# The queries' length as a scale of the scores: forget-bias and latent heads of a three-block transformer

## The chip, the cores and the metric

The kernel runs on one core of a Trainium2 chip. The metric is the device time of one launch in microseconds (us), as the median of several runs. A core has a matrix engine (TensorE, PE), a vector engine (VectorE, DVE), a scalar engine (ScalarE, ACT), a general engine (GpSimd, POOL) and a queue engine that issues the DMAs here (SyncE, SP). The engines run side by side and wait for one another through semaphores.

## The reference

Three blocks work on 512 tokens of width 1024 in fp32. The first is an even mixer (eight forget-bias heads and eight chunked heads with a relative bias) with an MLP, the second an odd mixer (eight stick-breaking heads and eight latent heads) with an MLP, the third a hybrid mixer with a gated MLP. The change touches the forget-bias heads of the first block and the latent heads of the second. Both work on inputs that an RMS norm has scaled token by token:

```python
def rmsnorm(x, g):
    y = x * rsqrt(mean(x * x, axis=-1) + EPS)     # one factor per token
    return y * g

# forget-bias heads: h = rmsnorm(x, norm_mix), q = h @ Wq, k = h @ Wk
s = q @ k.T * HEAD_DIM ** -0.5
s = s + cum_q[:, None] - cum_k[None, :]           # cum: running sum of log forget gates
p = softmax(where(k_pos <= q_pos, s, -inf))
o = p @ v

# latent heads: q_full = rmsnorm(c_q, q_norm) @ w_uq, kv = rmsnorm(c_kv, kv_norm) @ w_ukv
s = (q_nope @ k_nope.T + rope(q_rope) @ rope(k_rope).T) * (NOPE_DIM + ROPE_DIM) ** -0.5
p = softmax(where(k_chunk <= q_chunk, s, -inf))   # chunks of 64 tokens
o = p @ v
```

The factor of the norm is one number for each token. In the scores it is one number for each row (the query's token) and one for each column (the key's token).

## The kernel before, in words

Activations lie feature-major, as tiles of 128 features by 512 tokens. Every fp32 operand of a matrix product is kept as a high and a low part (`wh`, `wl` of a weight, an `AB` pair of an activation), and a product is three passes: high by high, high by low, low by high. `split` (L574) makes such a pair: ACT copies the high part, and DVE subtracts it from the source to get the low part.

The norm's factor is not applied to the input of a projection but to its result. `rows` (L670) turns a column of factors, one per token, into a 128x512 tile that holds the factors along the tokens (`rbc`, and `rbcq` with the scores' scale in it): PE transposes the broadcast column, four times for 512 tokens, and ACT copies the result from PSUM. `scaled_pair` (L708) multiplies a projection's result in PSUM by that row on DVE, into a tile `G`, and splits `G` into a pair `AB`. There are two buffers `AB` and three `G`. SP then moves the pair by DMA to where the scores want it: `to_stack` (into `QS`), `to_dup` (into `KK`), and for the latent heads `mla_operands` (L1003, into tiles `h`, with the roped part `X` and the key's `krp` beside it).

`softmax` (L745) handles 128 queries at a time against 128, 256, 384 or 512 keys. PE makes the scores in PSUM (`pss`). One DVE instruction, the bias-and-maximum, adds the bias or mask (`strip`) to the scores and takes the extremum of each row (the scores are negated here, so it is a minimum); it shows in the trace as a custom instruction with a read of its accumulator behind it. ACT takes the exponential and its sum, DVE the reciprocal, and POOL multiplies by it (`x<-x,sm`). Then PE transposes the probabilities (`psp`), they are split (`pt`) and multiplied by the values (`pso`).

A forget-bias head makes its own bias (`fox_bias`, L890): PE transposes the running sums, ACT copies them, and for each block of queries POOL adds the query's sum, a per-partition pointer, and fills what lies above the diagonal (`affine_select`). A latent head has one mask for all (`chm`, L1043). `latent_rows` (L982) makes the rows of the latent keys and queries, lets POOL multiply the rope's cosine and sine tiles by the queries' row, and runs the rope's projection.

The order of the instructions is not the program's. Every operation is recorded, and a list scheduler (`schedule`, L391) places them by assumed costs (`cost`, L322) and latencies, with priority by place in the program; `later` and `fill` push pieces of other work (the latent inputs, half of an output projection) between the heads. A tile gets a buffer in the order in which the operations are placed (`BUFS`, L544; PSUM `PBUFS`, L546). All recorded operations are issued from one line, so the trace shows L372 for each of them, and groups are told apart by their tiles: `psg` is a projection's result, `wr` a weight as loaded, `sm` a small column of factors, sums or maxima, `L` and `o` the latent inputs of queries and keys.

Of the kernel before, what the change touches and what calls it, by code (L numbers as in the profile page):

```python
# [15 lines left out]
ALU = mybir.AluOpType  # L16
# [4 lines left out]
NT = 4  # L21
KD = 8
BIG = 1e30
# [479 lines left out]
class Net:  # L503
# [204 lines left out]
    def scaled_pair(self, ps, rbc):  # L708
        t = self.tl("G", [128, 512])
        self.nc.vector.tensor_tensor(t, ps, rbc, ALU.mult)  # L710
        ab = self.pair("AB")
        self.split(ab, t)
        return ab
# [31 lines left out]
    def softmax(self, i, passes, bias, gate=None):  # L745

        nc = self.nc
        n = 128 * (i + 1)
        s = self.scores(i, passes)
        p = self.tl("x", [128, 512])  # L750
        m = self.small(4)
        nc.vector.tensor_tensor_reduce(p[:, :n], s[:, :n], bias(i), scale=1.0, scalar=3e38,
                                       op0=ALU.add, op1=ALU.min, accum_out=m[:, 0:1])
        nc.scalar.activation(p[:, :n], p[:, :n], AF.Exp, scale=-1.0, bias=m[:, 0:1], accum_out=m[:, 1:2])
        nc.vector.reciprocal(m[:, 2:3], m[:, 1:2])
        if gate == "raw":
            return p, m[:, 2:3]
        nc.gpsimd.tensor_scalar(p[:, :n], p[:, :n], m[:, 2:3], 1.0 if gate is None else gate(i), ALU.mult, ALU.mult)
        return p
# [60 lines left out]
    def soft_head(self, passes, bias, v, dst, u, gate=None):  # L820
        ps_list = [self.softmax(i, passes, bias, gate) for i in range(NT)]
        pt = self.turn(ps_list)
        o = self.psum("o")
        self.av(o, pt, v)
        self.fold(o, dst, u)
# [36 lines left out]
    def even_mixer(self):  # L862
        nc = self.nc
        rbc, rbcq = self.finish_norm([("rbc", 1.0), ("rbcq", -0.125)])
# [19 lines left out]
        for a in range(NT):  # L884
            nc.tensor.matmul(ps[:, 8 * a:32], allones if a else tri, lf[:, 0:32 - 8 * a], start=(a == 0), stop=(a == NT - 1))
        cum, ncum = self.small(32), self.small(32)
# [3 lines left out]
        def fox_bias(hd):  # L890
# [7 lines left out]
            def bias(i):  # L898
                n = 128 * (i + 1)
                b = self.tl("strip", [128, 512])  # L900
                nc.gpsimd.tensor_scalar(b[:, :n], ck[:, :n], ncum[:, 8 * i + hd:8 * i + hd + 1], 1.0, ALU.add, ALU.mult)
                nc.gpsimd.affine_select(b[:, n - 128:n], b[:, n - 128:n], pattern=[[-1, 128]], compare_op=ALU.is_ge,
                                        fill=BIG, base=0, channel_multiplier=1)
                return b[:, :n]
# [11 lines left out]
        for kind, mk in (("fox", fox_bias), ("chk", chk_bias)):  # L916
            for t in range(4):
                if not (kind == "fox" and t == 0) and t % 2 == 0:
                    vt = self.v_tiles(f"{kind}_v{t // 2}", h, self.rcol)
                q, k = self.qk(f"{kind}_qk{t}", h, rbcq, rbc, "op" if kind == "fox" and t == 0 else "gg")  # L920
# [7 lines left out]
                for u in range(2):  # L928
                    passes = [(qs[:, u], kk[u][:, 0]), (qs[:, u], kk[u][:, 1])]
                    self.soft_head(passes, mk(2 * t + u), self.vhead(vt, 2 * (t % 2) + u), ob, u)  # L930
# [5 lines left out]
    def odd_mixer(self):  # L936
# [45 lines left out]
        def latent_rows():  # L982

            rkb, = self.rows(lat["rkv"], [("rbc", 1.0)])
            rqb, = self.rows(lat["rq"], [("rbcq", -(96.0 ** -0.5))])
            nc.gpsimd.tensor_tensor(C, C, rqb, ALU.mult)
            nc.gpsimd.tensor_tensor(S, S, rqb, ALU.mult)
# [8 lines left out]
            return rkb, rqb, hold["r"]  # L996
# [6 lines left out]
        def mla_operands(t):  # L1003
            q = qkd(f"uq_nope{t}", lat["cq"], rqb)
# [16 lines left out]
        for t in range(4):  # L1021
# [8 lines left out]
            if t == 3:  # L1030
                with self.rec.later(LATER):
                    vm = self.v_tiles("ukv_v0", lat["ckv"], lat["rkv"])
                    rkb, rqb, (r1, r2) = latent_rows()
# [11 lines left out]
        nc.gpsimd.memset(chm[0:64, 448:512], BIG)  # L1045
        for t in range(4):
# [4 lines left out]
            for u in range(2):  # L1051
                Q, K = pair[u]
                passes = [(Q[0:96, 0], K[0:96, 0]), (Q[0:96, 0], K[0:96, 1]), (Q[0:96, 1], K[0:96, 0])]
                self.soft_head(passes, lambda i: chm[:, 384 - 128 * i:512], self.vhead(vt, 2 * (t % 2) + u), ob, u)
# [736 lines left out]
```

## Time and profile before

| | |
|---|---|
| runs | 2073.0, 2075.69, 2075.41 us; median 2075.41 |
| profiled execution | 2075.91 us, of which the span from first to last instruction 2074.2 us |
| mean granted TensorE clock | 0.991 |
| TensorE matmuls | 2016.1 us, 97% of the span |
| TensorE weight loads | 1684.7 us, 81%, beside the matmuls |
| VectorE | 1134.4 us, 55% |
| ScalarE | 895.1 us, 43% |
| GpSimd | 394.3 us, 19% |

Busy time is a mean over the whole span. What matters for a change is the stretch in which it lies, and there which engine waits for which. In the rows below, a bracket at the end of a row gives how long the engine had been idle and what released it.

### The profile page before, as it was taken

The numbers are of one execution on the slowest core, as the hardware profiler recorded it, in microseconds if no ns is written. First come the engines' busy times: TensorE is split into PE (matmuls) and PEld (weight loads), VectorE is DVE, ScalarE is ACT, GpSimd is POOL, SyncE is SP. The second block draws the span as 40 slices with busy tenths as digits, with TensorE's granted clock in tenths as the row PEclk, the third lists the DMA queues.
The fourth block names the chain that finished last, engine by engine and source line by source line (L and its number), as shares of the span: only waits on it lengthen the run. The fifth ranks groups of instructions, "written<-read, shape, count | busy, mean of one in ns | idle before, by whom it ended". The sixth has DMA issues, their size and how long they took to land. (4 is left out here: it accounts for less than half of the span.)

```text
span 2074.2 us, 27227 instructions
## 1 busy us (share of the span) xinstructions
PE 2016.1 (97%) x9958; PEld 1684.7 (81%) x9958; DVE 1134.4 (55%) x2033; ACT 895.1 (43%) x1621; POOL 394.3 (19%) x524
## 2 busy tenths in 40 slices
PE   8999999999999998999999999989999999999998
PEld 7887778888888887878888888867788888888887
DVE  6657763434444677874434354766786644333334
ACT  5556542323344565652323253534685543222224
POOL 2343210000022453220000014212240221011013
PEclk9999999999999999999999999999999999999999
DMA  6545623233344325633333334464113222323232
GB/s 199 135 128 152 195 83 102 92 102 92 101 134 132 102 62 130 194 101 96 97 100 94 102 120 141 119 174 126 60 42 112 92 101 92 102 92 102 91 102 82
DMA packets 80677, 231.98 MB, mean 112 GB/s; under 512 B 11552, under 2 KB 15520, under 8 KB 80544
## 3 DMA queue, kind: packets, MB, share of 16 engines
q1 hardware_dynamic: 80544, 230.25, 36.8%
q8 instruction: 78, 1.28, 0.3%
q14 instruction: 55, 0.45, 0.1%
HBM read 183.04 MB, written 10.49 MB: 93 GB/s over the span
## 5 line engine op out<-in xcount | busy, mean ns | idle before, releaser
L372 PE MATMUL psg<-h,wh 128*128 128x512 f32 x2688 | 847.3, 393 | 1.0 <-ACT h L372 0.6
L372 ACT ACTIVATE wh<-wr 128x1024 fp32r<-128x1024 f32 (+3 forms) x313 | 326.2, 1042 | 847.8 <-PE psg L372 679.1
L372 PEld LDWEIGHTS psg<-h,wh 128*128 128x128 f32 x2688 | 503.4, 189 | 101.4 <-ACT h L372 1.1
L372 PE MATMUL psg<-h,wl 128*128 128x512 f32 x1344 | 528.6, 393 | 0.9 <-DVE wl L372 0.7
L372 DVE TENSOR_TENSOR wl<-wr,wh 128x1024 fp32r<-128x1024 f32 (+3 forms) x313 | 385.7, 1233 | 60.7 <-ACT wh L372 59.6
L372 PEld LDWEIGHTS psg<-h,wl 128*128 128x128 f32 x1344 | 253.7, 189 | 53.1 <-DVE wl L372 2.4
L372 DVE TENSOR_TENSOR x<-psg,x 128x512 f32<-128x512 f32 (+1 forms) x120 | 78.1, 654 | 281.9 <-PE psg L372 281.9
L372 PE MATMUL psg<-KK,wh 128*128 128x512 f32 (+1 forms) x752 | 226.3, 382 | 0.0
L372 POOL TENSOR_TENSOR acc<-acc,T 128x512 f32<-128x512 f32 (+1 forms) x50 | 73.5, 1470 | 776.6 <-issue 629.1
L372 PE MATMUL psg<-V,wh 128*128 128x512 f32 (+1 forms) x656 | 200.4, 386 | 0.0
L372 PEld LDWEIGHTS psg<-KK,wh 128*128 128x128 f32 x752 | 140.0, 188 | 27.5
L372 PE MATMUL psg<-KK,wl 128*128 128x512 f32 (+1 forms) x376 | 143.8, 382 | 0.0
L372 PEld LDWEIGHTS psg<-V,wh 128*128 128x128 f32 x656 | 122.8, 188 | 25.0
L372 DVE SCALAR_TENSOR_TENSOR T<-psg,rbc 128x512 f32<-128x512 f32 x64 | 44.3, 692 | 167.8 <-PE psg L372 167.2
L372 PE MATMUL psg<-o,wh 128*128 128x512 f32 x400 | 131.8, 399 | 3.4 <-DVE AB L372 1.5
L372 ACT ACTIVATE x<-x,sm 128x128 f32<-128x128 f32 (+1 forms) x192 | 106.5, 558 | 55.9 <-DVE sm L372 55.5
L372 PE MATMUL psg<-V,wl 128*128 128x512 f32 (+1 forms) x328 | 126.7, 386 | 0.0
L372 PE MATMUL psg<-wh,h 128*128 128x256 f32 (+2 forms) x560 | 113.8, 290 | 6.9 <-ACT wh L372 6.8
L372 PE MATMUL pso<-pt,V 128*128 128x128 f32 (+3 forms) x432 | 108.1, 337 | 2.7 <-ACT pt L372 1.3
L372 POOL TENSOR_SCALAR x<-x,sm 128x128 f32<-128x128 f32 (+1 forms) x112 | 65.4, 589 | 178.5 <-DVE sm L372 100.2
L372 PEld LDWEIGHTS psg<-wh,h 128*128 128x128 f32 x560 | 91.6, 193 | 8.8 <-ACT wh L372 6.8
L372 POOL TENSOR_TENSOR T<-T,rbc 128x512 f32<-128x512 f32 x22 | 39.2, 1781 | 280.5 <-ACT T L372 280.5
(267 smaller groups left out, 2701.4 us busy)
## 6 DMA issues: line engine op xcount, KB each, us to landing
wr<-in_w_dram SPq DMA_DIRECT2D x302, 512.0 KB, 3.5
KK<-AB SPq DMA_DIRECT2D x48, 256.0 KB, 5.6
QS<-AB SPq DMA_DIRECT2D x48, 128.0 KB, 3.8
x<-xs SPq DMA_DIRECT2D x24, 256.0 KB, 3.3
xs<-P SPq DMA_DIRECT2D x16, 256.0 KB, 3.5
xs<-x SPq DMA_DIRECT2D x16, 256.0 KB, 2.0
h<-AB SPq DMA_DIRECT2D x16, 256.0 KB, 3.8
KK<-AB SPq DMA_DIRECT2D x32, 128.0 KB, 2.3
```

Source lines behind the costliest of these rows:

```text
L372: op.inst = getattr(getattr(nc, op.eng), op.name)(*op.args, **op.kw)
```

## The change

The queries of the forget-bias and of the latent heads are no longer multiplied by their row of factors. `scaled_pair` gets `None` for the row and splits the projection's result straight from PSUM. The factor, with the scores' scale and the sign in it, is kept as a 128x4 tile `qcol`, one column for each block of 128 queries, and goes into the bias-and-maximum as a per-partition pointer for its `scale`. That scale multiplies the bias too, so the forget bias on POOL is multiplied by the inverse (`qinv`, a second pointer in an instruction that had an immediate), and the masks' fill changes its sign. `latent_rows` no longer makes the queries' row, and the cosine and sine tiles are used as they are. The chunked heads and the stick-breaking heads keep their rows.

```diff
--- before.py
+++ after.py
@@ -706,8 +706,10 @@
 
 
     def scaled_pair(self, ps, rbc):
-        t = self.tl("G", [128, 512])
-        self.nc.vector.tensor_tensor(t, ps, rbc, ALU.mult)
+        t = ps
+        if rbc is not None:
+            t = self.tl("G", [128, 512])
+            self.nc.vector.tensor_tensor(t, ps, rbc, ALU.mult)
         ab = self.pair("AB")
         self.split(ab, t)
         return ab
@@ -742,14 +744,14 @@
             nc.tensor.matmul(s[:, :n], st[:, 128 * i:128 * i + 128], mv[:, :n], start=(a == 0), stop=(a == len(passes) - 1))
         return s
 
-    def softmax(self, i, passes, bias, gate=None):
+    def softmax(self, i, passes, bias, gate=None, scale=None):
 
         nc = self.nc
         n = 128 * (i + 1)
         s = self.scores(i, passes)
         p = self.tl("x", [128, 512])
         m = self.small(4)
-        nc.vector.tensor_tensor_reduce(p[:, :n], s[:, :n], bias(i), scale=1.0, scalar=3e38,
+        nc.vector.tensor_tensor_reduce(p[:, :n], s[:, :n], bias(i), scale=1.0 if scale is None else scale[:, i:i + 1], scalar=3e38,
                                        op0=ALU.add, op1=ALU.min, accum_out=m[:, 0:1])
         nc.scalar.activation(p[:, :n], p[:, :n], AF.Exp, scale=-1.0, bias=m[:, 0:1], accum_out=m[:, 1:2])
         nc.vector.reciprocal(m[:, 2:3], m[:, 1:2])
@@ -817,8 +819,8 @@
         self.gemm(key, mov, evac, tags)
         return res
 
-    def soft_head(self, passes, bias, v, dst, u, gate=None):
-        ps_list = [self.softmax(i, passes, bias, gate) for i in range(NT)]
+    def soft_head(self, passes, bias, v, dst, u, gate=None, scale=None):
+        ps_list = [self.softmax(i, passes, bias, gate, scale) for i in range(NT)]
         pt = self.turn(ps_list)
         o = self.psum("o")
         self.av(o, pt, v)
@@ -883,6 +885,10 @@
 
         for a in range(NT):
             nc.tensor.matmul(ps[:, 8 * a:32], allones if a else tri, lf[:, 0:32 - 8 * a], start=(a == 0), stop=(a == NT - 1))
+
+        qcol, qinv = self.tl("lam", [128, 4]), self.tl("rcol", [128, 4])
+        nc.vector.tensor_scalar(qcol, self.rcol, -0.125, None, ALU.mult)
+        nc.vector.reciprocal(qinv, qcol)
         cum, ncum = self.small(32), self.small(32)
         nc.vector.tensor_scalar(cum, ps[:, 0:32], 1.0, None, ALU.mult)
         nc.vector.tensor_scalar(ncum, ps[:, 0:32], -1.0, None, ALU.mult)
@@ -898,9 +904,9 @@
             def bias(i):
                 n = 128 * (i + 1)
                 b = self.tl("strip", [128, 512])
-                nc.gpsimd.tensor_scalar(b[:, :n], ck[:, :n], ncum[:, 8 * i + hd:8 * i + hd + 1], 1.0, ALU.add, ALU.mult)
+                nc.gpsimd.tensor_scalar(b[:, :n], ck[:, :n], ncum[:, 8 * i + hd:8 * i + hd + 1], qinv[:, i:i + 1], ALU.add, ALU.mult)
                 nc.gpsimd.affine_select(b[:, n - 128:n], b[:, n - 128:n], pattern=[[-1, 128]], compare_op=ALU.is_ge,
-                                        fill=BIG, base=0, channel_multiplier=1)
+                                        fill=-BIG, base=0, channel_multiplier=1)
                 return b[:, :n]
 
             return bias
@@ -917,7 +923,7 @@
             for t in range(4):
                 if not (kind == "fox" and t == 0) and t % 2 == 0:
                     vt = self.v_tiles(f"{kind}_v{t // 2}", h, self.rcol)
-                q, k = self.qk(f"{kind}_qk{t}", h, rbcq, rbc, "op" if kind == "fox" and t == 0 else "gg")
+                q, k = self.qk(f"{kind}_qk{t}", h, rbcq if kind == "chk" else None, rbc, "op" if kind == "fox" and t == 0 else "gg")
                 qs = self.to_stack(q)
                 kk = self.to_dup(k)
                 if kind == "chk":
@@ -927,7 +933,8 @@
                 ob = self.T()
                 for u in range(2):
                     passes = [(qs[:, u], kk[u][:, 0]), (qs[:, u], kk[u][:, 1])]
-                    self.soft_head(passes, mk(2 * t + u), self.vhead(vt, 2 * (t % 2) + u), ob, u)
+                    self.soft_head(passes, mk(2 * t + u), self.vhead(vt, 2 * (t % 2) + u), ob, u,
+                                   scale=qcol if kind == "fox" else None)
                 ops.append(self.finish_pair(ob))
         self.rec.flush()
         self.out_proj("out_ab1", ops[4:], "mlp0")
@@ -982,9 +989,9 @@
         def latent_rows():
 
             rkb, = self.rows(lat["rkv"], [("rbc", 1.0)])
-            rqb, = self.rows(lat["rq"], [("rbcq", -(96.0 ** -0.5))])
-            nc.gpsimd.tensor_tensor(C, C, rqb, ALU.mult)
-            nc.gpsimd.tensor_tensor(S, S, rqb, ALU.mult)
+
+            qcol = self.tl("lam", [128, 4])
+            nc.vector.tensor_scalar(qcol, lat["rq"], -(96.0 ** -0.5), None, ALU.mult)
             hold = {}
 
             def rope_evac(m, ps):
@@ -993,7 +1000,7 @@
                     hold["r"] = self.rope(hold[0], ps, C, S, "X4")
 
             self.gemm("uq_rope", lat["cq"], rope_evac)
-            return rkb, rqb, hold["r"]
+            return rkb, qcol, hold["r"]
 
         def qkd(key, ops_, bc):
             got = []
@@ -1001,7 +1008,7 @@
             return got[0]
 
         def mla_operands(t):
-            q = qkd(f"uq_nope{t}", lat["cq"], rqb)
+            q = qkd(f"uq_nope{t}", lat["cq"], None)
             k = qkd(f"ukv_k{t}", lat["ckv"], rkb)
             res = []
             for u in range(2):
@@ -1030,7 +1037,7 @@
             if t == 3:
                 with self.rec.later(LATER):
                     vm = self.v_tiles("ukv_v0", lat["ckv"], lat["rkv"])
-                    rkb, rqb, (r1, r2) = latent_rows()
+                    rkb, qcol, (r1, r2) = latent_rows()
                     first = mla_operands(0)
             ob = self.T()
             for u in range(2):
@@ -1042,7 +1049,7 @@
         vt = vm
         chm = self.tl("strip", [128, 512])
         nc.gpsimd.memset(chm, 0.0)
-        nc.gpsimd.memset(chm[0:64, 448:512], BIG)
+        nc.gpsimd.memset(chm[0:64, 448:512], -BIG)
         for t in range(4):
             if t == 2:
                 vt = self.v_tiles("ukv_v1", lat["ckv"], lat["rkv"])
@@ -1051,7 +1058,7 @@
             for u in range(2):
                 Q, K = pair[u]
                 passes = [(Q[0:96, 0], K[0:96, 0]), (Q[0:96, 0], K[0:96, 1]), (Q[0:96, 1], K[0:96, 0])]
-                self.soft_head(passes, lambda i: chm[:, 384 - 128 * i:512], self.vhead(vt, 2 * (t % 2) + u), ob, u)
+                self.soft_head(passes, lambda i: chm[:, 384 - 128 * i:512], self.vhead(vt, 2 * (t % 2) + u), ob, u, scale=qcol)
             self.fill(half, OUT1[t + 1], FILL1)
             ops.append(self.finish_pair(ob))
         self.rec.flush()
```

The change also alters the scheduler's order. It does so in the forget-bias stretch and at the latent heads; elsewhere the order is the same.

On DVE at the start of the latent heads, before the change (`G<-psg,rbcq` is a query's product, `G<-psg,rbc` a key's, `AB<-G,AB` their splits, `X` the rope's, `ISA` the bias-and-maximum and the read of its accumulator):

```order
L372 TENSOR_TENSOR G_1476<-psg_1472,rbcq_1460 128x512
L372 TENSOR_TENSOR G_1482<-psg_1478,rbc_1458 128x512
L372 TENSOR_TENSOR X_1399_1471<-G_1469,X_1399_1471 128x512
L372 TENSOR_TENSOR AB_1477<-G_1476,AB_1477 128x512
L372 TENSOR_TENSOR AB_1483<-G_1482,AB_1483 128x512
L372 TENSOR_TENSOR G_1598<-psg_1594,rbcq_1460 128x512
L372 TENSOR_TENSOR wl_1603<-wr_1601,wh_1602 128x256
L372 TENSOR_TENSOR wl_1589<-wr_1587,wh_1588 128x1024
L372 TENSOR_TENSOR G_1604<-psg_1600,rbc_1458 128x512
L372 ISA x_1543,sm_1544<-pss_1542,strip_1540 128x128
L372 ISA sm_1544 128x1
```

The same place on DVE after the change (`AB_1473` and `AB_1594` are the first and the second query's splits, `lam_1457` is `qcol`):

```order
L372 TENSOR_TENSOR AB_1473<-psg_1469,AB_1473 128x512
L372 TENSOR_TENSOR G_1478<-psg_1474,rbc_1456 128x512
L372 TENSOR_TENSOR wl_1598<-wr_1596,wh_1597 128x256
L372 TENSOR_TENSOR X_1396_1468<-G_1466,X_1396_1468 128x512
L372 TENSOR_TENSOR AB_1479<-G_1478,AB_1479 128x512
L372 TENSOR_TENSOR G_1599<-psg_1595,rbc_1456 128x512
L372 TENSOR_TENSOR wl_1585<-wr_1583,wh_1584 128x1024
L372 TENSOR_TENSOR AB_1594<-psg_1590,AB_1594 128x512
L372 ISA x_1539,sm_1540<-pss_1538,strip_1536,lam_1457 128x128
L372 ISA sm_1540 128x1
L372 ISA x_1542,sm_1543<-pss_1541,strip_1536,lam_1457 128x256
```

The two queries' products are gone, and the second query's split now stands ahead of the first bias-and-maximum, where before only the products of the second pair stood.

On SP at the same place, the first latent pair's moves before the change (`h_1484` is the first query's tile, `h_1485` the first key's, `h_1486` the second query's):

```order
L372 DMA h_1484<-X_1396_1468 16x1024
L372 DMA h_1485<-krp_1297 32x512 x2
L372 DMA h_1486<-X_1396_1468 16x1024
L372 DMA h_1484<-X_1399_1471 16x1024
L372 DMA h_1484<-AB_1477 64x1024
L372 DMA h_1485<-AB_1483 64x1024
L372 DMA h_1486<-AB_1477 64x1024
L372 DMA h_1486<-X_1399_1471 16x1024
```

The same place on SP after the change (`h_1480`, `h_1481` and `h_1482` in the same roles):

```order
L372 DMA h_1480<-X_1393_1465 16x1024
L372 DMA h_1480<-AB_1473 64x1024
L372 DMA h_1481<-krp_1295 32x512 x2
L372 DMA h_1480<-X_1396_1468 16x1024
L372 DMA h_1481<-AB_1479 64x1024
L372 DMA h_1482<-AB_1473 64x1024
L372 DMA h_1482<-X_1393_1465 16x1024
L372 DMA h_1482<-X_1396_1468 16x1024
```

The first query's move of `AB` has come forward, ahead of the key's `krp` moves; the key's move of `AB` still stands behind the first query's.

## Rows read from the trace of the kernel before

**Rows 1.** The page's busy times: us, share of the span, instructions.

```profile
PE 2016.1 (97%) x9958; PEld 1684.7 (81%) x9958; DVE 1134.4 (55%) x2033; ACT 895.1 (43%) x1621; POOL 394.3 (19%) x524
```

**Rows 2.** Windows: stretch, us, PE PEld DVE ACT POOL busy, clock, DMA, GB/s.

```profile
30.00:172.00 142.00, 138.76 (x848) 119.82 (x846) 89.14 (x233) 78.57 (x184) 56.83 (x114) 1.00 0.52 138
...
780.00:835.00 55.00, 49.74 (x279) 40.68 (x278) 42.16 (x106) 31.40 (x78) 19.61 (x27) 1.00 0.53 134
835.00:895.00 60.00, 56.18 (x281) 45.92 (x280) 50.18 (x117) 34.88 (x78) 11.09 (x17) 0.97 0.59 177
849.00:853.00 4.00, 3.91 (x16) 3.46 (x17) 3.14 (x11) 2.56 (x7) 0.43 (x2) 0.69 0.85 311
```

**Rows 3.** PE's waits, 30 to 172 us: total us, times, longest.

```profile
PE psp L372 <- POOL x L372: 1.0, 2, 0.8
PE pss L372 <- DMA KK<-AB: 0.8, 1, 0.8
```

**Rows 4.** PE's timeline, 789 to 791 us: start, us, instructions.

```profile
789.94 0.71 PE L372 MATMUL pss<-cst,sm 128*128 128x128 f32 x5
790.40 0.70 PE L372 MATMUL psg<-L,wh 128*128 128x512 f32 x2
```

**Rows 5.** DVE's instruction groups, 20 to 300 us: busy us, mean ns | idle before.

```profile
L372 DVE SCALAR_TENSOR_TENSOR V<-psg,sm,V 128x256 fp32r<-128x256 f32 x15 | 7.1, 478 | 1.6 <-ACT V L372 1.4
L372 DVE TENSOR_TENSOR pt<-psp,pt 128x256 fp32r<-128x256 f32 x16 | 6.7, 418 | 1.9 <-ACT pt L372 1.8
...
L372 DVE TENSOR_TENSOR G<-psg,rbcq 128x512 f32<-128x512 f32 x7 | 4.8, 684 | 5.6 <-PE psg L372 5.6
```

**Rows 6.** POOL's instruction groups, whole span.

```profile
L372 POOL TENSOR_SCALAR x<-x,sm 128x512 f32<-128x512 f32 x28 | 21.4, 766 | 29.0 <-DVE sm L372 20.9 <-PE psp L372 4.9 <-PE pso L372 2.8
L372 POOL TENSOR_SCALAR x<-x,sm,gt 128x512 f32<-128x512 f32 x16 | 15.2, 949 | 15.8 <-PE psp L372 9.2 <-DVE sm L372 5.2 <-PE pso L372 1.4
...
L372 POOL TENSOR_SCALAR x<-x,sm 128x128 f32<-128x128 f32 x28 | 11.5, 411 | 104.7 <-DVE sm L372 41.9 <-PE psg L372 34.8 <-PE pss L372 28.0
...
L372 POOL TENSOR_SCALAR x<-x,sm,gt 128x128 f32<-128x128 f32 x16 | 7.4, 465 | 40.9 <-DVE sm L372 40.4 <-PE psg L372 0.5
```

**Rows 7.** PE's timeline at the start of the latent heads, 800 to 812 us.

```profile
802.99 0.49 PE L372 MATMUL psg<-o,wh 128*128 128x512 f32 x1 [1.54 <-DVE AB L372]
...
803.99 0.50 PE L372 MATMUL psg<-o,wl 128*128 128x512 f32 x1 [0.50 <-DVE wl L372]
...
807.84 0.93 PE L372 MATMUL pss<-h,h 96*128 96x128 f32 x6 [0.81 <-issue]
...
810.97 0.96 PE L372 MATMUL pss<-h,h 96*128 96x512 f32 x3 [0.74 <-DVE sm L372]
```

**Rows 8.** DVE's timeline at the same place, 798 to 813 us.

```profile
798.22 1.78 DVE L372 TENSOR_TENSOR X<-G,X 128x512 fp32r<-128x512 f32 x1
...
801.12 0.68 DVE L372 TENSOR_TENSOR X<-G,X 128x512 fp32r<-128x512 f32 x1
...
808.40 0.29 DVE L372 CUSTOM_DVE_ANT_0 x<-pss,strip 128x128 f32<-128x128 f32 x1 [2.49 <-PE pss L372]
...
809.88 0.69 DVE L372 TENSOR_TENSOR AB<-G,AB 128x512 fp32r<-128x512 f32 x1 [1.17 <-ACT AB L372]
810.49 0.42 DVE L372 CUSTOM_DVE_ANT_0 x<-pss,strip 128x256 f32<-128x256 f32 x1
```

**Rows 9.** ACT's timeline at the same place, 801 to 811 us.

```profile
801.88 1.06 ACT L372 ACTIVATE wh<-wr 128x1024 fp32r<-128x1024 f32 x1
809.21 0.63 ACT L372 ACTIVATE AB<-G 128x512 fp32r<-128x512 f32 x1 [6.28 <-DMA h<-AB]
```

**Rows 10.** SP's queue at the same place, 800 to 806 us.

```profile
803.22 1.91 SPq L372 DMA_DIRECT2D h<-AB  x3
```

**Rows 11.** POOL's timeline, 797.7 to 800 us.

```profile
797.91 1.54 POOL L372 TENSOR_TENSOR G<-G,G 128x512 f32<-128x512 f32 x1 [0.29 <-DVE G L372]
```

**Rows 12.** PE's timeline at the third latent pair, 846 to 850 us.

```profile
849.09 0.93 PE L372 MATMUL pss<-h,h 96*128 96x128 f32 x6 [2.18 <-DMA h<-AB]
```

## The prediction

> **What bounds the kernel now.** I read the page's busy times first, then the stretches in which the change works, then what TensorE waits for in them, then single instructions. TensorE (PE) is busy 97% of the span, VectorE (DVE) 55%, ScalarE (ACT) 43% and GpSimd (POOL) 19% [rows 1]. So time can be won in two ways only: PE does less, or it waits less. The changed code lies in two stretches. In the forget-bias heads, 30 to 172 us, PE is busy 138.76 of 142.00 us, which leaves 3.24 us of idle time. In the latent heads it leaves 5.26 us of 55.00 (the start, 780 to 835) and 3.82 us of 60.00 (835 to 895) [rows 2]. At full clock these three numbers, 12.3 us, are all that a change off PE can win.
>
> Of the 3.24 us, 0.8 us is one wait for the keys' transfer `KK<-AB`, and the keys are not touched; 1.0 us is two waits for POOL's normalised probabilities [rows 3]. Queries are not in that list: their transfers land before the keys', which are issued behind them.
>
> **The change part by part.**
>
> *Four transposes on PE.* The row of the latent queries' length took four of the five matmuls that stand together at 789.94; the next group begins at 790.40 [rows 4], so five take 0.46 us and four of them 0.37, say 0.4 us. PE is without a wait there, so this is won in full: −0.4.
>
> *Eight products on DVE.* Each 128x512 product with the row took 0.684 us [rows 5], together 5.5 us. In the fox heads the product stands between the query's matmuls and its split, but the key's product, split and two transfers come behind it and are late last. So a query that is ready 0.7 us sooner releases nothing there: 0. The split then reads PSUM rather than SBUF. I take that at no difference for DVE (the product that reads PSUM took 0.684, the split from SBUF 0.69 at 809.88 [rows 5, 8]); the cover is the key again.
>
> *The scale as a pointer in 64 bias-and-maximum instructions.* No such instruction with a pointer for the scale is in the trace. The nearest pair of rows is, at 256 columns and from PSUM, 478 ns with a per-partition pointer and 418 without [rows 5]: +60 ns, 3.8 us over 64. From above, POOL's second pointer at 512 columns costs 183 ns [rows 6], 11.7 us over 64; from below 0, or less if a pointer were cheaper than an immediate, for which no row speaks. I take 60 ns, the same engine. Per head that is 4 x 0.06 = 0.24 us.
>
> *Three four-column instructions on DVE.* No more than the smallest bias-and-maximum, 0.29 us [rows 8], each: under 0.9 us, long before their first reader. DVE as a whole then does 5.5 − 3.8 − 0.9 = 0.8 us less. It is busy 89.14 of 142.00 us in the fox stretch [rows 2]; none of this is counted.
>
> *The second pointer in POOL's forget bias.* POOL's product with one pointer takes 411 ns at 128 columns and 766 at 512; with two 465 and 949 [rows 6]: +54 and +183. The four widths of a head at the mean of these ends, 0.12 us, give 0.47 us a head, 3.8 us over eight. POOL is busy 56.83 of 142.00 us there [rows 2]. I count 0, since the bias of a head is made while PE works on another head. If that cover is gone, it is a rival below.
>
> *Two POOL products and one copy less* before the latent rope. They feed the rope, whose last step is late on DVE for another reason: the first `X<-G,X`, at 798.22, took 1.78 us and the second 0.68 [rows 8], while POOL ran a product from 797.91 to 799.45 [rows 11], and that product stays. I count 0; if the whole rope came sooner, the gain would lie within the 3.59 us of the latent start below.
>
> The Trainium skill's page "SBUF — State Buffer", section "Who interferes with whom", says that a DVE instruction with two SBUF inputs and a GpSimd instruction that reads SBUF share a port, and that the later one waits for the whole of the other. The trace agrees: 1.78 against 0.68 us [rows 8, 11]. It speaks against the change in the fox heads, since POOL's longer biases would hold DVE's weight splits by as much again, up to 3.8 us; against that, the queries' split has one SBUF input now, and falls out of the lock. It would add to the slower rival, and not to the sum.
>
> *The order at the start of the latent heads.* This is the only place where I expect PE's waits to shift. PE waits there 1.54 us for DVE (`AB`; behind it ACT's copy of the weights `wh`, which ends at 802.94), 0.50 for `wl`, 0.81 before the first scores and 0.74 for a maximum [rows 7, 9]: 3.59 us. The first wait stays, since its last releaser is a weight copy that does not move. The 0.81 is the key's transfer: SP issues three moves of `AB` from 803.22 in 1.91 us [rows 10], 0.64 each; in the new order one of the queries' three goes before the key's other moves, and DVE has one product (0.68) fewer ahead of the key, so the key is under way 0.64 us earlier. One matmul of 512 columns now comes behind the scores and not before, so that PE arrives sooner by 0.49 us at most [rows 7]; about 0.4 of the 0.81 goes.
>
> Then something new stands in the way. In the new order DVE has the split of the *second* query, `AB_1594<-psg_1590`, ahead of the first bias-and-maximum. It needs ACT's copy into that `AB`, and ACT's copy waited 6.28 us for the buffer's transfer and ran at 809.21 [rows 9]. 0.64 us earlier that is 808.57; with 0.63 on ACT and 0.69 on DVE [rows 8, 9] the first bias-and-maximum starts at about 809.9, against 808.40 before. The second follows at 809.9 + 0.29 + 0.08 = 810.3, against 810.49 before, because before the change the same split stood between the two [rows 8]. PE's 0.74 us wait at 810.97 is for a maximum of this chain, and would end 0.2 us sooner. So I take −0.2 us for the whole place. Bounds: −3.6 (all four waits gone) and +1.5 (the first maximum's 809.9 − 808.40 passed on in full).
>
> *Later latent pairs.* The longest wait is 2.18 us at 849.09, for a transfer into `h` [rows 12]. It is the key's, which is issued after the query's and depends on a weight that is not moved: 0. Behind it the granted clock is 0.69 over 849 to 853 [rows 2], so part of that stretch ran at 1.2 GHz rather than 2.4; 4.00 x 0.31 = 1.24 us. I let both stand.
>
> **Sum.** The profiled execution took 2075.91 us (span 2074.2). 2075.91 − 0.4 − 0.2 = 2075.3. That execution lies 0.50 above the median of the runs shown, 2075.41, so the median should be 2074.8 us.
>
> **The rivals.**
>
> *A: faster, the latent start comes clear.* If the product less on DVE lets the whole chain pass before PE arrives, the 3.59 us go, and if the shorter stall at 849.09 leaves the clock up, 1.24 more: −0.4 − 3.6 − 1.2 = −5.2, 2070.2 us. For it: every one of the four waits ends on DVE or a transfer that DVE feeds [rows 7]. Against it: the first ends on a weight copy, and the AB buffer's transfer holds ACT as before [rows 9].
>
> *B: slower, the pointers lengthen every head's chain.* Scores, bias and maximum, exponential, reciprocal, normalisation and transposes follow one another, and the bias must be there first. Fully on the path, the pointers cost 8 x (0.24 + 0.47) = 5.7 us in the fox heads and 8 x 0.24 = 1.9 in the latent ones: 7.6 − 0.6 = +7.0, 2082.4 us. It decides (over 4.15 us slower) from 62% of the 7.6 on. For it: PE already waits for POOL's `x` [rows 3]. Against it: in two places of eight heads only, for 1.0 us; a quarter of 7.6 is 1.9, and gives 2074.8 + 1.9 = 2076.7.
>
> *C: nothing but the four transposes shows,* and the latent start gives its 0.2 back: 2075.0 us; with the new wait passed on in full, 2076.5.
>
> **How the numbers follow.** My forecast, with C at its side, has 0.61; a partial B, up to 4.15 us, 0.15; A 0.13; a B that decides 0.11. Two executions of this kernel can be told apart from about 0.2%, 4.15 us. So: faster 0.13, the same 0.76, slower 0.11. The range goes from 2071.0 (the start's waits all gone, 2074.8 − 3.6 rounded) to 2078.0 (a partial B of 40%, 7.6 x 0.4 = 3.0, on top of 2074.8).
>
> **What would show it.** Right: PE has four transposes fewer and 790 us comes 0.4 sooner; idle time in the fox stretch stays near 3.2 us; first latent scores about 0.6 us earlier against what precedes them, and the first bias-and-maximum later than the scores by over 2 us, behind the split of `AB_1594`. DVE's bias-and-maximum is some 60 ns longer, POOL's strip instruction 50 to 180. Wrong: waits for POOL's strip or `x` that grow by more than 2 us in the fox heads, a granted clock below 1.00 in a stretch where it was full, or a first latent wait that is gone.

## The result, and the profile after

| | before | after |
|---|---|---|
| median | 2075.41 us | 2087.86 us (2084.78 to 2091.18, 5 runs) |
| ratio | | 1.0073, 95% interval 1.0056 to 1.0091 |
| profiled execution, its span | 2075.91, 2074.2 us | 2084.78, 2083.1 us |
| mean granted TensorE clock | 0.991 | 0.991 |

The change made the kernel slower: 0.73% of 2075 is 15 us (11.6 to 18.9). The forecast was 2074.8 us, and no change. The profiled execution shows 8.9 us more; its mean clock is the same although it has a fall that the one of before has not (below), so it holds fewer falls elsewhere.

The page after has four transposes fewer on PE, as its count shows, yet PE is busy longer, not idle longer:

```profile
PE 2027.5 (97%) x9954; PEld 1684.4 (81%) x9954; DVE 1130.7 (54%) x2028; ACT 895.6 (43%) x1620; POOL 393.0 (19%) x522
```

PE has 11.4 us more of busy time with four instructions less [rows 1], and two things make it up.

**Slower matmuls, far from the change.** These are lines of part 5 of the page before (busy us, mean ns): down-projections of the MLPs and products of the third block, whose moving operand lies in `KK` or `V`.

```profile
L372 PE MATMUL psg<-KK,wh 128*128 128x512 f32 (+1 forms) x752 | 226.3, 382 | 0.0
...
L372 PE MATMUL psg<-V,wh 128*128 128x512 f32 (+1 forms) x656 | 200.4, 386 | 0.0
...
L372 PE MATMUL psg<-KK,wl 128*128 128x512 f32 (+1 forms) x376 | 143.8, 382 | 0.0
...
L372 PE MATMUL psg<-V,wl 128*128 128x512 f32 (+1 forms) x328 | 126.7, 386 | 0.0
```

The same lines of the page after:

```profile
L372 PE MATMUL psg<-KK,wh 128*128 128x512 f32 (+1 forms) x752 | 228.7, 385 | 0.0
...
L372 PE MATMUL psg<-V,wh 128*128 128x512 f32 (+1 forms) x656 | 202.9, 390 | 0.0
...
L372 PE MATMUL psg<-KK,wl 128*128 128x512 f32 (+1 forms) x376 | 144.9, 385 | 0.0
...
L372 PE MATMUL psg<-V,wl 128*128 128x512 f32 (+1 forms) x328 | 128.2, 391 | 0.0
```

The same 2112 matmuls took 2.4 + 2.5 + 1.1 + 1.5 = 7.5 us more. No wait stands before them, as the 0.0 at the end of each line says. In the first MLP the clock is full and PE never idle in either kernel, so that the count of matmuls shows their rate. 400 to 600 us, before:

```profile
400.00:600.00 200.00, 200.00 (x884) 165.58 (x884) 84.74 (x95) 63.54 (x79) 4.65 (x3) 1.00 0.32 101
```

The same stretch, after:

```profile
400.00:600.00 200.00, 200.00 (x876) 164.13 (x875) 82.98 (x94) 62.56 (x78) 1.81 (x1) 1.00 0.32 100
```

In 200 us 876 matmuls, not 884. PE's timeline tells which. A round of a down-projection is 24 matmuls, four `KK` and four `V` tiles with three passes each, and begins with the first `KK,wh`. Before:

```profile
324.58 0.62 PE L372 MATMUL psg<-KK,wh 128*128 128x512 f32 x2
...
330.02 0.62 PE L372 MATMUL psg<-KK,wh 128*128 128x512 f32 x2
```

After:

```profile
329.88 0.63 PE L372 MATMUL psg<-KK,wh 128*128 128x512 f32 x2
...
335.41 0.63 PE L372 MATMUL psg<-KK,wh 128*128 128x512 f32 x2
```

A round took 5.44 us and takes 5.53: from 227 to 230.5 ns a matmul. A round of the up-projections, whose moving operand is `h`, takes 5.44 us in both.

**Waits and a slow clock at the end of the forget-bias heads.** The stretch 155 to 170 us, before:

```profile
155.00:170.00 15.00, 13.89 (x93) 12.04 (x93) 12.15 (x44) 12.48 (x35) 8.15 (x17) 1.00 0.55 150
```

The same stretch, after:

```profile
155.00:170.00 15.00, 11.82 (x56) 8.65 (x56) 8.85 (x35) 8.15 (x25) 7.21 (x18) 0.77 0.43 118
```

PE does 56 matmuls instead of 93, and the granted clock is 0.77: for part of the stretch 1.2 GHz rather than 2.4, which costs at most 15.00 x 0.23 = 3.4 us (less where PE waits in it). Shorter windows show when. After, 155 to 160 and 160 to 167 us:

```profile
155.00:160.00 5.00, 2.84 (x13) 1.53 (x13) 2.50 (x11) 1.85 (x7) 3.45 (x9) 1.00 0.33 73
160.00:167.00 7.00, 5.98 (x20) 4.16 (x20) 3.65 (x13) 3.98 (x12) 3.17 (x7) 0.52 0.58 173
```

Before, 155 to 160 us:

```profile
155.00:160.00 5.00, 4.13 (x29) 3.47 (x29) 2.45 (x10) 2.53 (x8) 2.78 (x6) 1.00 0.91 244
```

PE was busy for 2.84 of 5.00 us ahead of the fall, where it had been for 4.13. Its timeline, ahead of the fall (up to 159.85) and in the slow stretch:

```profile
155.95 1.14 PE L372 MATMUL pss<-KK,QS 128*128 128x384 f32 x4 [0.60 <-DVE sm L372]
157.81 0.89 PE L372 MATMUL psp<-cst,x 128*128 128x128 f32 x3 [0.73 <-POOL x L372]
159.18 0.44 PE L372 MATMUL pss<-KK,QS 128*128 128x128 f32 x2 [0.47 <-DVE sm L372]
159.85 0.73 PE L372 MATMUL pss<-KK,QS 128*128 128x256 f32 x2 [0.23 <-DVE sm L372]
160.87 0.69 PE L372 MATMUL psp<-cst,x 128*128 128x128 f32 x2 [0.30 <-POOL x L372]
161.75 0.69 PE L372 MATMUL psp<-cst,x 128*128 128x128 f32 x2 [0.19 <-POOL x L372]
162.98 0.79 PE L372 MATMUL pso<-pt,V 128*128 128x512 f32 x1 [0.53 <-ACT pt L372]
```

Seven short waits, 3.05 us, 2.03 of them ahead of the fall, with no other work placed between them: the other work that stood here before had been placed earlier. The waits of 30 to 180 us grew accordingly, from 2.8 us in all to 4.9 [rows 3]:

```profile
PE psp L372 <- POOL x L372: 1.9, 5, 0.7
PE pss L372 <- DVE sm L372: 1.3, 3, 0.6
```

A landmark tells the cost of the stretch: the first scores of the third chunked pair. As many matmuls stand ahead of them as before, and from there to the latent heads PE's order is that of before. Before and after:

```profile
200.22 0.70 PE L372 MATMUL pss<-KK,QS 128*128 128x128 f32 x4 [1.25 <-DMA KK<-AB]
```

```profile
206.82 0.69 PE L372 MATMUL pss<-KK,QS 128*128 128x128 f32 x4 [0.86 <-DMA KK<-AB]
```

They come 6.6 us later. The waits and the slow clock make up 5.5 us of that at most; for the rest, PE is busy longer with the same matmuls in another order.

### The profile page after: what moved, and what is told of

Its sections match the earlier page's. It is cut to its first block, busy times and chain, and to the rows that moved or that the text cites. A ratio compares the mean times of both kernels' runs of the same rounds, so it can differ in the third digit from the quotient of the medians.

```text
span 2083.1 us, 27208 instructions
## 1 busy us (share of the span) xinstructions
PE 2027.5 (97%) x9954; PEld 1684.4 (81%) x9954; DVE 1130.7 (54%) x2028; ACT 895.6 (43%) x1620; POOL 393.0 (19%) x522
## 5 line engine op out<-in xcount | busy, mean ns | idle before, releaser
L372 ACT ACTIVATE pt<-psp 128x512 fp32r<-128x512 f32 (+3 forms) x176 | 70.4, 435 | 52.3 <-PE psp L372 50.2
```

The costliest lines, as they stand in the source:

```text
L372: op.inst = getattr(getattr(nc, op.eng), op.name)(*op.args, **op.kw)
```

## The experiments

Each kernel was timed against the kernel before on the same chip. An address is that which the built program gives a tile, in bytes of a partition.

**First set: is it the chip, the tiles' places, or the heads?** The change makes two tiles, `lam` and `rcol`, which existed later in the program, before the first `AB`. In the built program all that is made behind them (`G`, `AB`, `QS`, `KK`, `strip`, `pt`, `o`, `X4`, `L`) lies 64 bytes higher; `G` and `AB` also change places; the weights, `h` and `V` stay.

`c0_before_again` is the kernel before, unchanged. 

> The kernel before, unchanged, on the chip of this job. Theory C (the chip): the profile after came from a chip on which the down-projections' matmuls with moving tiles V and KK run at 228 to 235 ns from start to start, not at 227; then this run shows them too, at 4 to 5 ns more, and a span of some 2080 us. Theories A (addresses) and B (longer chains in the heads): 227 ns in the MLP stretch as in the first profile, ratio 1.000 within 0.002.

`c1_shift_only`, on top of before, the result not used:

```diff
+        qcol, qinv = self.tl("lam", [128, 4]), self.tl("rcol", [128, 4])
+        nc.vector.tensor_scalar(qcol, self.rcol, -0.125, None, ALU.mult)
+        nc.vector.reciprocal(qinv, qcol)
         cum, ncum = self.small(32), self.small(32)
```

> The kernel before with nothing of the change but its two four-column tiles, made at the same place (two small DVE instructions, their result not used). They come ahead of all later tiles in SBUF, so that G, AB, QS, KK, strip, pt, o, X4 and L lie 64 bytes higher, as after the change; V, h and the weights stay. Theory A (the slower matmuls of the down-projections come from where KK and its neighbours now lie): 230 to 235 ns for moving V and KK in the MLP, ratio 1.003 to 1.007. Theories B and C: 227 ns or the same as the repeat of the kernel before; ratio 1.000 within 0.002.

`c2_addresses_kept`, on top of the change:

```diff
-        qcol, qinv = self.tl("lam", [128, 4]), self.tl("rcol", [128, 4])
+        cum, ncum = self.small(32), self.small(40)
+        qcol, qinv = ncum[:, 32:36], ncum[:, 36:40]
...
-            qcol = self.tl("lam", [128, 4])
+            qcol = self.small(32)[:, 0:4]
```

> The whole change, but the scale and its inverse lie in unused columns of tiles that exist already (the 32-column sums of the forget gates, and one of the same size in the latent heads), so that QS, KK, strip, pt, o, X4 and L lie where they lay before; only G and AB still change places. Theory A: 227 ns in the MLP, and what is left of the 1.0073 is the heads' own, ratio 0.999 to 1.003. Theory B (the pointers and the new order in the heads): ratio 1.005 to 1.008 as after the change. Theory C: the same as after, 1.007, on a chip whose repeat of before shows 230 ns and more.

| | ratio (95%) | round | clock, 155 to 170 us | landmark |
|---|---|---|---|---|
| c0_before_again | 1.0012 (0.9995 to 1.0029) | 5.44 us | 1.00 | 200.71 us |
| c1_shift_only | 1.0060 (1.0041 to 1.0078) | 5.53 us | 1.00 | 201.43 us |
| c2_addresses_kept | 1.0037 (1.0021 to 1.0053) | 5.44 us | 0.77 | 206.89 us |

A round of c1 begins at each of these lines:

```profile
321.78 0.63 PE L372 MATMUL psg<-KK,wh 128*128 128x512 f32 x2
...
327.31 0.63 PE L372 MATMUL psg<-KK,wh 128*128 128x512 f32 x2
```

Two small tiles and nothing else of the change, in an order that is otherwise that of before, cost 0.6%. This is theory A, and theory C (the chip) is out. The change without the shift still costs 0.37%, a little over the range that theory A alone gave, and shows the slow clock. So there are two causes, in different places. Their costs, 0.60% and 0.37%, add up to more than the 0.73% of the whole; the intervals (0.41 to 0.78 and 0.21 to 0.53) allow for that.

**Second set: which part of the change in the heads?** All with the tiles where they lay. `e3_fox_only` and `e4_latent_only` are `c2_addresses_kept` with the latent or the forget-bias heads as before; `e5_pointers_only` is the kernel before with these edits:

```diff
+        nc.vector.tensor_scalar(qcol, self.rcol, 0.0, 1.0, ALU.mult, ALU.add)
+        nc.vector.reciprocal(qinv, qcol)
...
-  ... ncum[:, 8 * i + hd:8 * i + hd + 1], 1.0, ALU.add, ALU.mult)
+  ... ncum[:, 8 * i + hd:8 * i + hd + 1], qinv[:, i:i + 1], ALU.add, ALU.mult)
```

and with `scale=qcol` in the bias-and-maximum of these heads. `e7_estimate` is `c2_addresses_kept` with one edit in `cost`, which the scheduler reads:

```diff
         if op.name == "tensor_scalar":
+            if self.tag.get(self.region(out)[0]) == "strip":
+                k = min(k, 1)
             return 160 + 0.836 * n + 83 * k
```

> The change in the forget-bias heads alone; the latent heads as before; tiles where they lay before (scale and inverse in unused columns), so 227 ns in the MLP. What is left of the change with kept addresses (1.0037 there) lies in the heads. Theory O (the order: the scheduler's estimate charges POOL's bias 83 ns for its second pointer and so puts other matmuls earlier, and TensorE has nothing to do at the end of the forget-bias heads, at 159 to 163 us) and theory P (the pointers' own time): 1.002 to 1.004, with the waits for DVE sm and POOL x, and a clock of 0.5 over some 6 us from 160 us. Theory L (the latent heads): 1.000.

> The change in the latent heads alone; the forget-bias heads as before; tiles where they lay before. Theory L: 1.002 to 1.004. Theories O and P: 1.000 within 0.0015, no fall of the clock at 160 us; the order at the start of the latent heads is that of the change, and TensorE's waits there stay about where they were in sum (within 1.5 us).

> Only the pointers of the forget-bias heads: scale and inverse are tiles of ones, and the queries are still multiplied by their row. TensorE's order is row by row that of the forget-bias change alone. Theories O and P: as the forget-bias change alone, 1.002 to 1.004, waits at 159 to 163 us and the clock at 0.5 behind them. If instead the lost products on DVE were to blame, 1.000 and no fall of the clock.

> The whole change with tiles kept where they lay, and the scheduler's estimate charges POOL's bias for one pointer as before, not for two. The pointers run all the same; the order in the forget-bias heads is another. Theory O: no fall of the clock at 160 us, waits in the forget-bias stretch back to about 2.8 us, ratio 0.999 to 1.001. Theory P: the waits for POOL x and DVE sm stay, 1.002 to 1.004.

| | ratio (95%) | clock, 155 to 170 us | landmark |
|---|---|---|---|
| e3_fox_only | 1.0039 (1.0023 to 1.0055) | 0.77 | 206.85 us |
| e4_latent_only | 0.9998 (0.9979 to 1.0017) | 1.00 | 200.82 us |
| e5_pointers_only | 1.0030 (1.0012 to 1.0048) | 0.66 | 207.70 us |
| e7_estimate | 1.0018 (0.9999 to 1.0037) | 1.00 | 204.89 us |

The latent heads show no cost (the interval ends at 0.17%, under the 0.2% that theory L asked for): theory L falls. The forget-bias heads carry all of it, and with ones in the pointers and the products kept (e5) it is the same: the lost products are not to blame. Up to the landmark PE's instructions come in e5 in the order of the change. e7 runs the same pointers in another order (neither that of the change nor that of before), and the clock stays up. 155 to 170 us of e7:

```profile
155.00:170.00 15.00, 13.14 (x97) 11.81 (x96) 9.10 (x35) 9.04 (x26) 6.50 (x16) 1.00 0.61 146
```

97 matmuls stand here again. So the order decides over the slow clock, as theory O has it: the five kernels with the order of the change (after, c2, e3, e5 and a17 below) all show the fall, and no other kernel does. But its waits did not go back to 2.8 us, as O had said they would, and its ratio, 1.0018, lies between the ranges of O and P. PE's waits of 30 to 175 us in e7 (the edit moves the line number by two) begin with

```profile
PE pss L374 <- DVE sm L374: 2.6, 4, 1.4
PE psp L374 <- POOL x L374: 1.2, 3, 0.6
```

which is 5.5 us in all, and the landmark stands between the two, 2.0 us sooner than in c2. The ratios of c2 and e7 alone can't be told apart: their intervals overlap. A part of P (the pointers' own time, or an order that is still worse than that of before) is not excluded.

**Third set: the tiles' places, against what?** On top of the kernel before; a pad is a tile that is written once and never read.

```diff
# a7_shift_128: as c1, and behind the two tiles
+        pad = self.tl("pad", [128, 16])
# a8_behind_KK: the two tiles of c1 behind the first to_dup
# a9_only_KK: the two tiles ahead of the first to_dup, the pad of 64 bytes behind it
# a10_with_V: the two tiles ahead of the first v_tiles
# a11_KK_2048: the first pt2 (2048 bytes) made ahead of the first to_dup
# a13_all: the pad ahead of x     a14_all_behind_weights: the pad ahead of acc
# a15_V_512: as a10, with a pad of 448 bytes behind the two tiles
```

> As the run that only shifts, with a third small tile of 64 bytes behind the two, so that G, AB, QS, KK, strip, pt, o, X4 and L lie 128 bytes higher than before instead of 64. Theory A1 (a start at an odd multiple of 64 bytes is what slows the matmuls): 227 ns for moving V and KK in the MLP, ratio 1.000 within 0.002. Theory A2 (any move of these tiles against V, h and the weights does it): 230 ns and more, 1.004 to 1.007.

> The two small tiles are made behind KK: strip, pt, o, X4 and L lie 64 bytes higher, while V, G, AB, QS and KK stay. Theory A1 for the moving tile itself: 227 ns in the MLP, whose moving tiles are h, V and KK. If a tile that PE doesn't read there decides: 230 ns and more.

> The two small tiles ahead of KK and a pad of 64 bytes behind it: KK alone lies 64 bytes higher, what follows 128, what precedes not at all. Theory A1 for the moving tile itself: KK at 229 to 235 ns and V at 227. If KK's place slows V too, as in the shift of all: V at 228 to 233 as well.

> The kernel before with the two small tiles made ahead of V: V, G, AB, QS, KK and all behind them lie 64 bytes higher together, h and the weights stay. Theory A3 (what counts is where KK lies against V, the two moving tiles that take turns in one down-projection): they are 38912 bytes, 19 x 2048, apart as before, so 227 ns in the MLP and 1.000 within 0.002. Theory A2 (any move of these tiles against h or the weights): 230 ns and more, 1.004 to 1.007.

> A tile of 2048 bytes that used to come later is made ahead of KK, so that KK lies 2048 bytes higher, 20 x 2048 from V; V, G, AB and QS stay, and from o on all lies as before. Theory A3 with the distance taken in steps of 2048 bytes: 227 ns for V and KK. If only the exact distance of before were good: 228 ns and more.

> The kernel before with a pad of 64 bytes ahead of everything: the weights, h, V and KK lie 64 bytes higher together. Theory A4 (what counts is where a moving tile lies against the weights wh and wl that are loaded beside it): 227 ns for h, V and KK. Theory A5 (the place itself, whatever the weights): V and KK at 229 ns on the mean, as when all from V on moved.

> The pad of 64 bytes behind the weights: h, V and KK lie 64 bytes higher, the weights stay. Theory A4: V and KK at 229 ns on the mean, and h slower than 227 in the up-projections too, for the first time. Theory A5 (the place itself): V and KK at 229; h as it may be.

> V and all behind it 512 bytes higher; h and the weights stay. A weight tile of one step is 512 bytes wide, so that against the weights V and KK lie as before but for whole steps. Theory A4 with the distance taken in steps of 512 bytes: 227 ns for V and KK. Theory A4 with steps of 2048 bytes: 228 ns and more.

The table sets the round against the distance of `V` and of `KK` from the weight tile `wh` (at 29568 before; `wl` is 36 x 256 behind it, and a step's weights 512 wide), as the rest after division by 256. Before, `h` is 104 x 256 away, `V` 279 x 256 and `KK` 431 x 256: no rest.

| | V | KK | round | time |
|---|---|---|---|---|
| before, c0, c2 | 0 | 0 | 5.44 us | |
| a8_behind_KK | 0 | 0 | 5.44 us | 2068.05 us, one run |
| a11_KK_2048 | 0 | 0 | 5.44 us | 2073.82 us, one run |
| a13_all | 0 | 0 | 5.44 us | 2071.64 us, one run |
| a15_V_512 | 0 | 0 | 5.44 us | 2076.79 us, one run |
| after, c1 | 0 | 64 | 5.53 us | 1.0073 and 1.0060 |
| a9_only_KK | 0 | 64 | 5.53 us | 2088.68 us, one run |
| a7_shift_128 | 0 | 128 | 5.53 us | 1.0046 (1.0027 to 1.0066) |
| a10_with_V | 64 | 64 | 5.49 us | 1.0022 (1.0006 to 1.0038) |
| a14_all_behind_weights | 64 | 64 | 5.49 us | 2086.18 us, one run |

The single runs are there for their rounds; one time says little, since the runs of the kernel before alone go from 2063.39 to 2083.17 us. A round of a13 begins at each of these lines:

```profile
322.20 0.62 PE L372 MATMUL psg<-KK,wh 128*128 128x512 f32 x2
...
327.64 0.62 PE L372 MATMUL psg<-KK,wh 128*128 128x512 f32 x2
```

A1 falls with a7, where `KK` starts at a multiple of 128 and is slow all the same. A2 falls with a11, where `KK` moved by 2048 bytes at no cost. A3 is half right: moved together, `V` and `KK` lose less, 5.49, but not nothing. A4 holds in all ten: no rest means 5.44. a13 tells A4 from A5: everything 64 bytes higher, and no loss. In a14, where the weights alone stay, `h` has a rest too, and for the first time the up-projections slow down, from 5.44 us a round to 5.49; a round of them begins at each of these lines:

```profile
360.04 0.62 PE L372 MATMUL psg<-h,wh 128*128 128x512 f32 x2
...
365.53 0.62 PE L372 MATMUL psg<-h,wh 128*128 128x512 f32 x2
```

a15 leaves steps of 512 bytes open. That 256 is enough is what `V` and `KK` of the kernel before say (odd multiples), and a17 below.

**Fourth set: both mended.** `a12_mended` is the change with its two tiles ahead of `V` and the estimate of e7. `a17_pad_only` is the change with a pad, and `a16_pad_256` adds the estimate:

```diff
         nc.vector.reciprocal(qinv, qcol)
+        pad = self.tl("pad", [128, 48])
+        nc.vector.memset(pad, 0.0)
```

> The whole change with its two tiles made ahead of V, so that all from V on lies 64 bytes higher together, and the scheduler's estimate charging POOL's bias for one pointer; the order is row by row that of the earlier run with this estimate. Theories A3 and O together: 227 ns in the MLP, no fall of the clock at 160 us, ratio 0.999 to 1.002. If the full move of the tiles also costs: 1.005 and more. It would beat the kernel before only by the four transposes, 0.4 us, which these runs can't tell.

> The whole change as it is, with 192 bytes of pad behind its two small tiles, so that KK and what follows move by 256 bytes and not 64, and with the estimate that charges POOL's bias for one pointer. Theory A4 with steps of 256 bytes, and theory O: 227 ns in the MLP, no fall of the clock at 160 us, ratio 0.999 to 1.002. If only steps of 512 bytes are good: KK and V at 229 ns and more, 1.004 to 1.007.

> The whole change as it is, order and all, with the 192 bytes of pad alone. Theory A4 with steps of 256 bytes: 227 ns in the MLP, and what is left is the order's share: the fall of the clock at 160 us, ratio 1.002 to 1.005. If the pad doesn't help: 1.0073 as the change itself.

| | ratio (95%) | round | clock, 155 to 170 us |
|---|---|---|---|
| a12_mended | 1.0050 (1.0033 to 1.0068) | 5.49 us | 1.00 |
| a17_pad_only | 1.0032 (1.0013 to 1.0051) | 5.44 us | 0.77 |
| a16_pad_256 | 1.0020 (1.0001 to 1.0038) | 5.44 us | 1.00 |

a12 missed its range, since its places were chosen by A3; a10's 0.22% and e7's 0.18% add up to 0.40%, within its interval. 192 bytes of pad, which make the shift 256, take the change from 0.73% to 0.32%, and the round back to 5.44. The stretch of a16 is busy again:

```profile
155.00:170.00 15.00, 14.56 (x107) 13.13 (x106) 10.64 (x38) 10.45 (x29) 7.41 (x17) 1.00 0.59 146
```

Neither beats the kernel before. The intervals of a17 and a16 overlap, so what the estimate is worth is read from the traces: the clock of 160 us, and the landmark, at 206.94 us in a17 and 203.71 in a16. With both causes mended some 4 us stay (0.2 to 7.9), whose cause no run here settles. e4 points to the forget-bias heads, and so does a16's trace: the landmark still comes 3.5 us later there than before, with a full clock, and PE's waits of 30 to 175 us are only 0.9 us more in sum (3.7 against 2.8). No run has the pointers in the order of before, so what of the 4 us is the order and what the pointers stays open.

## Why the prediction was wrong, point by point

**The step that failed first** is that the sum had no term for where tiles lie: "This is the only place where I expect PE's waits to shift" names all that was looked for, and outside the two stretches nothing was. About half of the loss or more is there: 7.5 us by the page's lines, 0.41% between the ratios of the change and of a17.

**The second** is "I count 0, since the bias of a head is made while PE works on another head". That took the order around the head as given. But the scheduler's estimate charges 83 ns for each pointer, and e5 and e7 show that this charge moved other matmuls forward and left the end of the stretch bare. The price of the second pointer itself is seen where nothing holds POOL up. One head before, the widths 128 and 256 in the first line and 384 and 512 in the second; the third line is an instruction of the next head:

```profile
58.20 0.82 POOL L372 TENSOR_SCALAR strip<-T,sm 128x128 f32<-128x128 f32 x2 [5.96 <-ACT T L372]
...
59.70 1.25 POOL L372 TENSOR_SCALAR strip<-T,sm 128x384 f32<-128x384 f32 x2 [0.19 <-DVE sm L372]
...
73.67 2.01 POOL L372 TENSOR_SCALAR strip<-T,sm 128x384 f32<-128x384 f32 x1 [0.19 <-DVE sm L372]
```

The same head after:

```profile
59.06 0.98 POOL L372 TENSOR_SCALAR strip<-T,sm,rcol 128x128 f32<-128x128 f32 x2 [5.86 <-ACT T L372]
...
60.80 1.42 POOL L372 TENSOR_SCALAR strip<-T,sm,rcol 128x384 f32<-128x384 f32 x2 [0.25 <-DVE sm L372]
```

That is 0.33 us more in this head. Over the eight heads the median instruction of each width is 74 to 80 ns longer, 0.30 us a head, where I had added 0.47. The means of the groups hide this, 2.57 us a head against 2.56 before, because a few instructions take some 1 us longer or more, as the one at 73.67 does: three of the 32 before, one after. The trace before had the same price: the groups of [rows 6] differ by 77 and 79 ns in their medians, and only their means by the 54 and 183 that I took. So the scheduler's 83 ns was nearly right. The order that came of it was worse all the same, by the clock's 3.4 us at most and some waits: without the charge the landmark comes 2.0 us sooner (e7 against c2) and 3.2 us sooner (a16 against a17).

**Rival B** (slower, 0.11) named the right heads and the right sign, 2082.4 us, but its mechanism, the pointers' time in full on the path, is not what the runs show. With the measured prices it would be 8 x (0.27 + 0.30) = 4.6 us of waits in the forget-bias heads; PE's waits of 30 to 175 us grew by 0.9 in a16 and by 2.7 in e7, which have the same pointers. In part it may be true of the 4 us that stay.

**What held.** The bias-and-maximum with a pointer:

```profile
L372 DVE CUSTOM_DVE_ANT_0 x<-pss,strip,lam 128x512 f32<-128x512 f32 x8 | 6.0, 747 | 0.0
L372 DVE CUSTOM_DVE_ANT_0 x<-pss,strip 128x512 f32<-128x512 f32 x8 | 5.4, 679 | 0.3 <-PE pss L372 0.2
```

+68 ns, where 60 were taken. POOL's instruction is longer by 74 to 80 ns, within the 50 to 180 named. At the latent start the second query's split comes first, as forecast, and the first bias-and-maximum 2.6 us after the first scores at 814.92:

```profile
816.90 0.69 DVE L372 TENSOR_TENSOR AB<-psg,AB 128x512 fp32r<-128x512 f32 x1 [4.10 <-ACT AB L372]
817.51 0.34 DVE L372 CUSTOM_DVE_ANT_0 x<-pss,strip,lam 128x128 f32<-128x128 f32 x1
```

PE's timeline there, from the place of the four transposes on:

```profile
798.16 0.27 PE L372 MATMUL pss<-cst,sm 128*128 128x128 f32 x1
798.18 0.70 PE L372 MATMUL psg<-L,wh 128*128 128x512 f32 x2
...
808.89 0.71 PE L372 MATMUL psg<-o,wh 128*128 128x512 f32 x2 [0.22 <-DVE AB L372]
...
811.21 1.25 PE L372 MATMUL psg<-o,wh 128*128 128x512 f32 x4 [0.27 <-ACT wh L372]
...
812.85 0.51 PE L372 MATMUL psg<-o,wl 128*128 128x512 f32 x1 [0.40 <-DVE wl L372]
...
814.92 0.93 PE L372 MATMUL pss<-h,h 96*128 96x128 f32 x6 [0.86 <-DMA h<-AB]
...
817.91 1.49 PE L372 MATMUL pss<-h,h 96*128 96x384 f32 x6 [1.14 <-DVE sm L372]
```

The transposes gave 0.44 us (0.02 from the one that is left to the next group, where five took 0.46 [rows 4]), as forecast. The first scores come 16.74 us behind that group, 0.70 sooner than before, where 0.6 was named, but not on the way that was named.

**What else failed, at the latent start.** "The first wait stays, since its last releaser is a weight copy that does not move" is wrong: PE waits for ACT's copy of `wh` for 0.27 us, where it had waited 1.54; no run here asks why. The wait before the scores, of which 0.4 us was to go, did not shrink, 0.86 us against 0.81 [rows 7], and the wait for a maximum grew from 0.74 to 1.14, where it was to shrink by 0.2. Together with the short wait ahead of them (0.21 at 800.75 before, 0.22 at 808.89 after) the waits of this place went from 3.80 us to 2.89; −0.2 had been taken. The wait at 849.09 has its answer in 2.42 us at 857.55 [rows 12]; e4's 0.9998 (0.9979 to 1.0017) shows no worth of the latent part either way.

## What to carry to other kernels

Compare the built program's tile addresses before and after a change, the smallest tile included: a tile made early moves everything behind it, and a kernel that is bound by TensorE pays for it in matmuls that the change never touched. Where a scheduler orders the work by estimates, ask what the change does to the order, even when the estimate of the changed instruction is right, and look at the stretch from which filling work is taken as well as at the one into which it goes. Take the price of an instruction from the median of a group, since a few that were held up move its mean. When a busy engine is busy longer with no more instructions, divide: the rate of a stretch without waits tells what no wait shows.

## What the runs showed of the hardware that I had not expected

A stream of 512-column fp32r matmuls runs at 227 ns from start to start when the moving tiles and the weight tiles lie a multiple of 256 bytes apart in the partition, and at 229 to 230.5 ns, as the mean of a round, when some or all of the moving tiles lie 64 or 128 bytes off (a round of 5.44 us against 5.49 to 5.53). The matmuls on `V`, whose own distance had no rest, slowed too when they shared a round with a shifted `KK`: the four groups of the page after show it. Why that is so, and what happens at other rests, no run here tells.
